# Queueing the modulation's column sums behind the LayerNorms of the sub-layer ahead

## The chip, the cores and the metric

The kernel runs on one core of a Trainium2 chip. The metric is the device time of one execution in microseconds (us); it is given as the median of several executions. The engines are TensorE (PE: matrix products and transposes, PEld its weight loads), VectorE (DVE), ScalarE (ACT), GpSimd (POOL) and SyncE (SP, whose queue issues most DMAs).

## What is computed

An encoder of two layers over 256 positions of width 1024, in float32, with a conditioning vector c. Layer 0 is feed-forward, gMLP, feed-forward; layer 1 is feed-forward, attention (against keys and values that are projected once from the stream), feed-forward. Each of the six sub-layers is, with w = 1/2 for the feed-forwards and 1 for the others,

```
x <- LayerNorm(ALPHA * x + w * gate(c) * f(x * (1 + scale(c)) + shift(c)))
```

`gate`, `scale` and `shift` are vectors of 1024 values each, `c` times columns of a large matrix `w_ada`. They make up twenty such vectors in all, K/V's two among them.

## The kernel before, in words

**Tiles and passes.** The 256 positions are two token tiles, t = 0 and 1, of 128. X[t] holds the residual stream. Every weight comes in pieces of 128 x 1024 in float32 (512 KB) from SP's queue (`load_raw`, L184) into one of six buffers of the pool `raw`. ScalarE makes the rounded part `hi` (L190) and VectorE the rest, `lo` (L191), into 11 `unit` buffers; each product is then three matmuls, `hi` by the activation's high part (L234), `lo` by it (L235), and `hi` by the activation's low part (L237). Only when `lo` has been written is the raw buffer free again. SP issues raw transfers in the program's order, and each waits for a released buffer.

**Columns.** The vectors of the modulation are sums over rows, one *column step* for each of eight pieces of 128 values: `column` (L122) loads 512 KB into the same pool `raw` and has VectorE multiply and reduce it in place, with a short read of the sum behind it. A list of these steps is set for each sub-layer by `ada_phase` (L158); `pump` (L166), called by `prep` (L194) for each weight piece that is prepared, takes steps from it by credits, so that columns lie between weights. Once a gate's eight columns are summed, `finish_gate` (L144) writes the sums to DRAM through POOL and reads them back as a broadcast tile `gate` on SP's queue (`small_dma`, L179).

**A sub-layer's end.** The last pass computes the two 512-wide halves of a tile. `add_y` multiplies a half with the gate (`gy`, L325) and adds it to X[t] (L327 or L330), `rstd_of` takes the statistics (`st` L338, `mv` L340, `rs` L342, and POOL's power, L343), and `normalise` (L346) applies them to both halves of X[t] (L349). The next sub-layer's input follows: TensorE transposes X (`hp`, L300), ScalarE scales and shifts it (`hf`, L288) and rounds it (`hh`, L269), VectorE makes the low part (`hl`, L270). Both tiles do this, tile 1 a little behind tile 0. The affine part of the LayerNorm is applied to X later (L368, L369).

**What sets the order.** No order is written out. The framework's planner takes the program in the order in which it is written as priorities, and puts each engine's instructions in a row by its own costs, by the dependences and by the buffers that are free. `tc.issue_after(i)` adds one more edge: the instructions inside it come behind `i` on the engine of `i`, which here is VectorE. The column steps of sub-layer s+1 begin while the weights of its first pass are prepared, so they reach into the last pass of sub-layer s.

The sub-layers are counted 0 to 5 below: FFN, gMLP, FFN, FFN, attention, FFN. "3 to 4" is the boundary between FFN and attention.

Of the kernel before, what the change touches and what calls it, by code (L numbers as in the profile page):

```python
# [11 lines left out]
ALU = mybir.AluOpType  # L12
# [32 lines left out]
LAG_R = (20, 16)  # L45

N_WARM = 40

COLS = [(0, 1), (0, 0), (0, 4), (0, 3), (0, 7), (0, 6), (1, 1), (1, 0), ("kv", 1), ("kv", 0),
        (1, 4), (1, 3), (1, 7), (1, 6)]  # L50
# [5 lines left out]
def encoder_kernel(ctx, tc, a, out):  # L56
    nc = tc.nc
# [22 lines left out]
    def nm(s):  # L80
        uid[0] += 1
        return f"{s}_{uid[0]}"
# [43 lines left out]
    def col_slice(key):  # L126
        ci = COLS.index(key)
        st = {}

        def step(j):  # L130
            if j == 0:
                st["m"] = modp.tile([P, KD], F32, tag="mod", name=nm("mod"))
            column(ci, j, st["m"])
            if j < KD - 1:
                return
            if ci < N_MODS:
                mods[key] = st["m"]
            else:
                after(LAG_M, lambda: finish_gate(key, st["m"]))
        return [lambda j=j: step(j) for j in range(KD)]  # L140
# [15 lines left out]
    ada = {"steps": [], "credit": 0.0}  # L156

    def ada_phase(*parts):  # L158

        for _, s in ada["steps"]:  # L160
            s()
        ada["steps"] = [(units / (KD * len(keys)), s) for keys, units in parts
                        for k in keys for s in col_slice(k)]
        ada["credit"] = 0.0

    def pump():  # L166
        ada["credit"] += 1.0
        while ada["steps"] and ada["credit"] >= ada["steps"][0][0]:
            cost, s = ada["steps"].pop(0)
            ada["credit"] -= cost  # L170
            s()


    last = {}
# [19 lines left out]
    def prep(srcs):  # L194
        w = split(load_raw(srcs), nc.vector)
        pump()
        return w
# [134 lines left out]
    def pieces(x_, cuts):  # L332
        return [x_[:, c0:c1] for c0, c1 in zip(cuts, cuts[1:])]

    def rstd_of(parts):
        stats = smp.tile([P, len(parts), 6], F32, tag=f"st{len(parts)}", name=nm("st"))
        for i, x_ in enumerate(parts):
            nc.vector.bn_stats(out=stats[:, i, :], in_=x_)  # L338
        mv = smp.tile([P, 2], F32, tag="mv", name=nm("mv"))
        nc.vector.bn_aggr(out=mv, in_=stats)  # L340
        rs = smp.tile([P, 2], F32, tag="rs", name=nm("rs"))
        nc.vector.tensor_scalar(rs[:, 0:1], mv[:, 1:2], EPS, None, op0=ALU.add)  # L342
        nc.gpsimd.tensor_tensor(rs[:, 1:2], rs[:, 0:1], mhalf, op=ALU.pow)  # L343
        return mv[:, 0:1], rs[:, 1:2]

    def normalise(t):  # L346
        mu, rs = rstd_of(pieces(X[t], HALVES))
        for x_ in pieces(X[t], HALVES):
            nc.vector.tensor_scalar(x_, x_, mu, rs, op0=ALU.subtract, op1=ALU.mult)  # L349

    lnrow = {}

# [25 lines left out]
    def end_sublayer(t, ln, nxt):  # L378

        normalise(t)  # L380
        hT[t] = []
        after(LAG_H[t], lambda: make_h(t, 0, nxt["mods"]))

        def second():
            make_h(t, 1, nxt["mods"])
            residual_affine(t, ln)
        after(LAG_H[t] + LAG_H2, second)
# [17 lines left out]
    def first_gu_part(w_gu, part, aT):  # L405
# [10 lines left out]
        warm = pt.tile([P, 512], F32, tag="pt", name=nm("warm"))  # L416
        for i in range(N_WARM):
            nc.tensor.transpose(warm[:, i % 4 * P:(i % 4 + 1) * P], ident, ident)
# [358 lines left out]
    def next_affine(ln, nxt, *keys):  # L777

        def f():
            ada_phase()  # L780
            flush()
            nxt["mods"] = [affine(mods[s_], mods[b_], ln) + dst
                           for (s_, b_), dst in zip(keys, ((htp, "h", hT), (bigp, "b", hkT)))]
            load_lnrow(ln)
        return f

    def step(ln):
# [3 lines left out]
    done, nxt = step(0)  # L791
    ffn(0, 0, (0, 2), done, next_affine(0, nxt, ((0, 4), (0, 3))), PARTS1,
        start=lambda: (ada_phase(([(0, 2)], 13), ([(0, 4), (0, 3)], 24)),))

    done, nxt = step(1)
    ada_phase(([(0, 5)], 16), ([(0, 7), (0, 6)], 22))
    gmlp((0, 5), done, next_affine(1, nxt, ((0, 7), (0, 6))))

# [63 lines left out]
```

## Time and profile before

| | us |
|---|---|
| median of 3 runs | 1055.06 (1053.86 to 1055.79) |
| the profiled execution | 1051.13 |
| its span | 1049.4 |

| engine | busy us | share of the span |
|---|---|---|
| TensorE | 1023.8 | 98% |
| VectorE | 848.0 | 81% |
| ScalarE | 506.1 | 48% |
| DMA engines (mean of 16) | | 77% |

TensorE's row is nearly full, so its stops are what can be shortened. A wait in the profile names the instruction that came last; the duration of an instruction with "xN" holds N of them. TensorE's matmuls overlap: one lists 0.39 us and the next starts 0.23 us later, so a stop is the time from one start to the next less 0.23 us.

### The profile page before, as it was taken

The numbers are of one execution on the slowest core, as the hardware profiler recorded it, in microseconds if no ns is written. First come the engines' busy times: TensorE is split into PE (matmuls) and PEld (weight loads), VectorE is DVE, ScalarE is ACT, GpSimd is POOL, SyncE is SP. The second block draws the span as 40 slices with busy tenths as digits, with TensorE's granted clock in tenths as the row PEclk, the third lists the DMA queues.
The fourth block names the chain that finished last, engine by engine and source line by source line (L and its number), as shares of the span: only waits on it lengthen the run. The fifth ranks groups of instructions, "written<-read, shape, count | busy, mean of one in ns | idle before, by whom it ended". The sixth has DMA issues, their size and how long they took to land.

```text
span 1049.4 us, 13511 instructions
## 1 busy us (share of the span) xinstructions
PE 1023.8 (98%) x4780; PEld 837.2 (80%) x4780; DVE 848.0 (81%) x1227; ACT 506.1 (48%) x710; POOL 22.4 (2%) x39
## 2 busy tenths in 40 slices
PE   8999999999999999999999999999999999999996
PEld 6778878887688788888878888887787788888885
DVE  6877887899999999988679986868998969655535
ACT  3554346462436454454456444453558556355520
POOL 0000000000000100000000000000000000000000
PEclk9999999999999999999999999999999999999999
DMA  8988899688799889999847996767898838645611
GB/s 325 388 324 324 303 361 332 234 277 284 248 344 332 276 279 326 373 348 325 296 149 264 330 349 232 252 242 265 285 341 291 290 102 274 228 161 197 244 61 40
DMA packets 111203, 285.74 MB, mean 272 GB/s; under 512 B 9888, under 2 KB 22560, under 8 KB 111136
## 3 DMA queue, kind: packets, MB, share of 16 engines
q1 hardware_dynamic: 110944, 284.86, 77.3%
q8 instruction: 37, 0.61, 0.2%
q14 instruction: 30, 0.25, 0.1%
q0 software_dynamic: 192, 0.02, 0.0%
HBM read 283.78 MB, written 1.07 MB: 271 GB/s over the span
## 4 chain that ended last, share of the span: by engine, by line
PE 71%; DVE 13%; DMA 7%; issue 4%; ACT 2%; POOL 1%; SPq 0%; POOLq 0%; DVEq 0%; ACTq 0%
PE acc L237 22%; PE acc L234 22%; PE acc L235 22%; DVE lo L191 3%; DMA raw<-w_cols 3%; DVE raw L122 3%; PE tp L276 2%; DMA raw<-ffn_gu 2%; DVE st L338 1%; DVE lo L449 1%; DMA raw<-w_in 1%; POOL rs L343 1%; DVE gy L325 1%; DMA raw<-w_o 1%; PE ob L737 1%
## 5 line engine op out<-in xcount | busy, mean ns | idle before, releaser
L190 ACT CAST hi<-raw 128x1024 fp32r<-128x1024 f32 x328 | 341.7, 1058 | 257.5 <-DMA raw<-ffn_gu 68.9
L191 DVE TENSOR_TENSOR lo<-raw,hi 128x1024 fp32r<-128x1024 f32 x328 | 394.7, 1220 | 54.8 <-ACT hi L190 49.7
L234 PE MATMUL acc<-hi,hh 128*128 128x512 f32 x924 | 359.4, 395 | 3.0 <-ACT hh L466 2.4
L235 PE MATMUL acc<-lo,hh 128*128 128x512 f32 x924 | 355.8, 392 | 5.3 <-DVE lo L191 4.6
L237 PE MATMUL acc<-hi,hl 128*128 128x512 f32 x924 | 291.1, 390 | 0.2 <-DVE hl L270 0.2
L122 DVE CUSTOM_DVE_ANT_0 raw<-raw,c_row,bcol 128x1024 f32<-128x1024 f32 x160 | 204.4, 1278 | 23.4 <-DMA raw<-w_cols 23.1
L235 PEld LDWEIGHTS acc<-lo,hh 128*128 128x128 f32 x924 | 173.0, 188 | 42.7 <-DVE lo L191 7.4
L234 PEld LDWEIGHTS acc<-hi,hh 128*128 128x128 f32 x924 | 173.2, 188 | 42.2 <-ACT hh L466 4.4
L237 PEld LDWEIGHTS acc<-hi,hl 128*128 128x128 f32 x924 | 173.2, 188 | 37.1 <-DVE hl L270 0.8
L234 PE MATMUL acc<-hi,th 128*128 128x512 f32 (+1 forms) x432 | 163.9, 387 | 0.2 <-ACT th L269 0.2
L235 PE MATMUL acc<-lo,th 128*128 128x512 f32 (+1 forms) x432 | 161.9, 383 | 0.1
L237 PE MATMUL acc<-hi,tl 128*128 128x512 f32 (+1 forms) x432 | 143.3, 383 | 0.0
L234 PEld LDWEIGHTS acc<-hi,th 128*128 128x128 f32 x432 | 81.2, 188 | 15.6 <-ACT th L269 0.5
L235 PEld LDWEIGHTS acc<-lo,th 128*128 128x128 f32 x432 | 81.1, 188 | 15.4 <-DVE lo L191 0.5
L237 PEld LDWEIGHTS acc<-hi,tl 128*128 128x128 f32 x432 | 80.6, 188 | 15.9
L395 DVE TENSOR_TENSOR a<-acc,sg 128x512 f32<-128x512 f32 (+1 forms) x48 | 30.9, 643 | 44.3 <-ACT sg L394 44.3
L394 ACT ACTIVATE sg<-acc 128x512 f32<-128x512 f32 (+1 forms) x48 | 27.0, 563 | 82.0 <-PE acc L237 79.9
L288 ACT ACTIVATE hf<-hp,B,A 128x128 f32<-128x128 f32 x96 | 36.7, 477 | 60.3 <-PE hp L300 60.3
L270 DVE TENSOR_TENSOR tl<-tp,th 128x512 fp32r<-128x512 f32 (+1 forms) x56 | 36.2, 649 | 26.5 <-ACT th L269 26.2
L269 ACT CAST th<-tp 128x512 fp32r<-128x512 f32 (+1 forms) x56 | 30.9, 554 | 52.4 <-PE tp L276 52.3
L325 DVE TENSOR_TENSOR gy<-acc,gate 128x512 f32<-128x512 f32 (+1 forms) x49 | 32.0, 675 | 20.5 <-PE acc L237 20.4
L343 POOL TENSOR_TENSOR rs<-rs,mhalf 128x1 f32<-128x1 f32 x14 | 14.7, 1053 | 674.0 <-DVE rs L342 674.0
(93 smaller groups left out, 539.3 us busy)
## 6 DMA issues: line engine op xcount, KB each, us to landing
raw<-w_cols SPq DMA_DIRECT2D x160, 512.0 KB, 5.3
raw<-ffn_gu SPq DMA_DIRECT2D x160, 512.0 KB, 5.5
raw<-ffn_down SPq DMA_DIRECT2D x88, 512.0 KB, 5.3
raw<-w_in SPq DMA_DIRECT2D x32, 512.0 KB, 5.2
raw<-ffn_gu SPq DMA_DIRECT2D x32, 256.0 KB, 4.2
raw<-w_out SPq DMA_DIRECT2D x16, 512.0 KB, 5.7
raw<-w_kv SPq DMA_DIRECT2D x16, 512.0 KB, 5.4
raw<-w_q SPq DMA_DIRECT2D x8, 512.0 KB, 4.7
```

What stands on the lines that cost most here:

```text
L122: nc.vector.tensor_tensor_reduce(out=raw, in0=raw, in1=c_row, scale=1.0, scalar=bcol[:, ci, j:j + 1], op0=ALU.mult, op1=ALU.add, accum_out ...
L190: nc.scalar.copy(hi, raw)
L191: last["lo"] = eng.tensor_tensor(lo, raw, hi.bitcast(F32), op=ALU.subtract)
L234: nc.tensor.matmul(acc, lhsT=xh, rhs=wh[:, sl], start=k == 0, stop=False)
L235: nc.tensor.matmul(acc, lhsT=xh, rhs=wl[:, sl], start=False, stop=False)
L237: nc.tensor.matmul(acc, lhsT=xl, rhs=wh[:, sl], start=False, stop=k == nk - 1)
L269: nc.scalar.copy(hi, src_ps)
L270: nc.vector.tensor_tensor(lo, src_ps, hi.bitcast(F32), op=ALU.subtract)
L288: nc.scalar.activation(hf[:, sl], tp[:, sl], AF.Identity, bias=B[:, j:j + 1], scale=A[:, j:j + 1])
L325: nc.vector.tensor_tensor(tmp, acc[:, :c1 - c0], g[:, sl], op=ALU.mult)
L394: nc.scalar.activation(sg[:, :wd], g, AF.Silu)
L395: nc.vector.tensor_tensor(av[:, :wd], u, sg[:, :wd], op=ALU.mult)
```

## The change

Column steps of a sub-layer get an extra edge, once the first sub-layer's LayerNorms have been recorded: the first two steps stand behind the second `normalise` instruction of tile 0 of the sub-layer ahead, all others behind that of tile 1. A counter of the steps is added to `ada_phase`, and `normalise` records its last instruction. The edge orders VectorE's reductions; the columns' transfers keep their places on SP.

```
+N_EARLY = 2
...
-        ada["credit"] = 0.0
+        ada["credit"], ada["n"] = 0.0, 0
...
             cost, s = ada["steps"].pop(0)
             ada["credit"] -= cost
-            s()
+            with ExitStack() as es:
+                if ("ln", 1) in last:
+                    es.enter_context(tc.issue_after(last["ln", ada["n"] >= N_EARLY].ins))
+                s()
+            ada["n"] += 1
...
         for x_ in pieces(X[t], HALVES):
-            nc.vector.tensor_scalar(x_, x_, mu, rs, op0=ALU.subtract, op1=ALU.mult)
+            last["ln", t] = nc.vector.tensor_scalar(x_, x_, mu, rs, op0=ALU.subtract, op1=ALU.mult)
```

The lines that follow are the planned rows of the engines. L-numbers are higher by two to six with the change, since lines were added. In the rows, a column is the `ISA` with `raw` and `mod`, with its short read behind it.

VectorE at tile 0's LayerNorm between sub-layers 1 and 2, before (X0 is the tile's stream, `st`, `mv` and `rs` its statistics):

```order
L122 ISA raw_710_3197,mod_694_3140<-raw_710_3197,c_row_102,bcol_108 128x1024
L122 ISA mod_694_3140 128x1
L340 BN_AGGR mv_669_3019<-st_668_3016 128x2
L122 ISA raw_714_3212,mod_694_3140<-raw_714_3212,c_row_102,bcol_108 128x1024
L122 ISA mod_694_3140 128x1
L342 TENSOR_SCALAR rs_670_3021<-mv_669_3019 128x1
L191 TENSOR_TENSOR lo_702_3168<-raw_700_3165,hi_701_3167 128x1024
L349 TENSOR_SCALAR X0_105<-X0_105,mv_669_3019,rs_670_3021 128x512 x2
L191 TENSOR_TENSOR lo_709_3194<-raw_707_3191,hi_708_3193 128x1024
```

and with the change:

```order
L346 BN_AGGR mv_669_3019<-st_668_3016 128x2
L348 TENSOR_SCALAR rs_670_3021<-mv_669_3019 128x1
L355 TENSOR_SCALAR X0_105<-X0_105,mv_669_3019,rs_670_3021 128x512 x2
L124 ISA raw_695_3141,mod_694_3140<-raw_695_3141,c_row_102,bcol_108 128x1024
L124 ISA mod_694_3140 128x1
L124 ISA raw_699_3156,mod_694_3140<-raw_699_3156,c_row_102,bcol_108 128x1024
L124 ISA mod_694_3140 128x1
L197 TENSOR_TENSOR lo_702_3168<-raw_700_3165,hi_701_3167 128x1024
```

Columns that stood between the statistics now stand behind the two instructions that normalise X0, and they are the first two of the gate's eight, 695 and 699; 710 and 714, which are later ones, are further down.

VectorE at tile 1's LayerNorm between sub-layers 3 and 4, before (`mod_1437` is the gate of the attention, `mod_1492` the vector after it, X1 tile 1's stream):

```order
L191 TENSOR_TENSOR lo_1469_6497<-raw_1467_6494,hi_1468_6496 128x1024
L340 BN_AGGR mv_1426_6362<-st_1425_6359 128x2
L191 TENSOR_TENSOR lo_1473_6512<-raw_1471_6509,hi_1472_6511 128x1024
L342 TENSOR_SCALAR rs_1427_6364<-mv_1426_6362 128x1
L191 TENSOR_TENSOR lo_1491_6619<-raw_1489_6616,hi_1490_6618 128x1024
L349 TENSOR_SCALAR X1_106<-X1_106,mv_1426_6362,rs_1427_6364 128x512 x2
L122 ISA raw_1493_6623,mod_1492_6622<-raw_1493_6623,c_row_102,bcol_108 128x1024
L122 ISA mod_1492_6622 128x1
L191 TENSOR_TENSOR lo_1496_6635<-raw_1494_6632,hi_1495_6634 128x1024
```

and with the change:

```order
L197 TENSOR_TENSOR lo_1469_6497<-raw_1467_6494,hi_1468_6496 128x1024
L348 TENSOR_SCALAR rs_1427_6364<-mv_1426_6362 128x1
L355 TENSOR_SCALAR X1_106<-X1_106,mv_1426_6362,rs_1427_6364 128x512 x2
L124 ISA raw_1446_6412,mod_1437_6381<-raw_1446_6412,c_row_102,bcol_108 128x1024
L124 ISA mod_1437_6381 128x1
L124 ISA raw_1450_6427,mod_1437_6381<-raw_1450_6427,c_row_102,bcol_108 128x1024
L124 ISA mod_1437_6381 128x1
L124 ISA raw_1458_6456,mod_1437_6381<-raw_1458_6456,c_row_102,bcol_108 128x1024
L124 ISA mod_1437_6381 128x1
L276 TENSOR_TENSOR hl_1454_6447<-hf_1452_6441,hh_1453_6446 128x512
L124 ISA raw_1462_6471,mod_1437_6381<-raw_1462_6471,c_row_102,bcol_108 128x1024
L124 ISA mod_1437_6381 128x1
```

One column of the next vector stood behind the normalise before; now six of the gate's stand there, four of them shown, and the low parts `lo_1473` and `lo_1491`, which stood ahead of it, come after five and six of them.

TensorE at the same boundary, before (`hp_1451` and `hp_1463` are the transposes of X1, `acc_1432` and `acc_1433` the accumulators of the key projection of tile 0):

```order
L237 MATMUL acc_1432_6373<-hi_1460_6467,hl_1057_4733 128x512
L237 MATMUL acc_1433_6374<-hi_1460_6467,hl_1057_4733 128x512
L234 MATMUL acc_1432_6373<-hi_1468_6496,hh_1056_4732 128x512
L235 MATMUL acc_1432_6373<-lo_1469_6497,hh_1056_4732 128x512
L234 MATMUL acc_1433_6374<-hi_1468_6496,hh_1056_4732 128x512
L235 MATMUL acc_1433_6374<-lo_1469_6497,hh_1056_4732 128x512
L237 MATMUL acc_1432_6373<-hi_1468_6496,hl_1057_4733 128x512
L237 MATMUL acc_1433_6374<-hi_1468_6496,hl_1057_4733 128x512
L234 MATMUL acc_1432_6373<-hi_1472_6511,hh_1056_4732 128x512
L235 MATMUL acc_1432_6373<-lo_1473_6512,hh_1056_4732 128x512
L300 MATMUL hp_1451_6436<-ident_109,X1_106 128x128 x4
L300 MATMUL hp_1463_6480<-ident_109,X1_106 128x128 x4
```

and with the change:

```order
L243 MATMUL acc_1432_6373<-hi_1456_6452,hl_1057_4733 128x512
L243 MATMUL acc_1433_6374<-hi_1456_6452,hl_1057_4733 128x512
L240 MATMUL acc_1432_6373<-hi_1460_6467,hh_1056_4732 128x512
L306 MATMUL hp_1451_6436<-ident_109,X1_106 128x128 x4
L241 MATMUL acc_1432_6373<-lo_1461_6468,hh_1056_4732 128x512
L240 MATMUL acc_1433_6374<-hi_1460_6467,hh_1056_4732 128x512
L241 MATMUL acc_1433_6374<-lo_1461_6468,hh_1056_4732 128x512
L243 MATMUL acc_1432_6373<-hi_1460_6467,hl_1057_4733 128x512
L243 MATMUL acc_1433_6374<-hi_1460_6467,hl_1057_4733 128x512
L306 MATMUL hp_1463_6480<-ident_109,X1_106 128x128 x4
L240 MATMUL acc_1432_6373<-hi_1468_6496,hh_1056_4732 128x512
```

The transposes of X1 stand two weight pieces earlier on TensorE than before: ahead of the products with `lo_1461`, where they stood among those with `hi_1472`.

## Rows read from the trace of the kernel before

**Rows 1.** The page: busy time of the engines, and the last chain by engine.

```profile
PE 1023.8 (98%) x4780; PEld 837.2 (80%) x4780; DVE 848.0 (81%) x1227; ACT 506.1 (48%) x710; POOL 22.4 (2%) x39
...
PE 71%; DVE 13%; DMA 7%; issue 4%; ACT 2%; POOL 1%; SPq 0%; POOLq 0%; DVEq 0%; ACTq 0%
```

**Rows 2.** Waits of TensorE: engine, line, waited for, total us, times, longest.

```profile
PE acc L235 <- DVE lo L191: 4.6, 3, 1.9
...
PE hp L300 <- DVE X L349: 2.5, 6, 0.8
...
PE acc L234 <- ACT hh L269: 0.2, 1, 0.2
PE acc L237 <- DVE hl L270: 0.2, 1, 0.2
```

**Rows 3.** Timeline of TensorE at 1 to 2: start, duration, instruction, idle before.

```profile
351.76 0.39 PE L234 MATMUL acc<-hi,th 128*128 128x512 f32 x1
352.74 1.09 PE L300 MATMUL hp<-ident,X 128*128 128x128 f32 x8 [0.59 <-DVE X L349]
```

**Rows 4.** Groups by line of VectorE: count, busy us, mean ns, idle before.

```profile
L191 DVE TENSOR_TENSOR lo<-raw,hi 128x1024 fp32r<-128x1024 f32 x328 | 394.7, 1220 | 54.8 <-ACT hi L190 49.7
L122 DVE CUSTOM_DVE_ANT_0 raw<-raw,c_row,bcol 128x1024 f32<-128x1024 f32 x160 | 204.4, 1278 | 23.4 <-DMA raw<-w_cols 23.1 <-DVE c_row L415 0.2
```

**Rows 5.** Waits of SP's own queue.

```profile
SPq L184 <- DVE lo L191: 261.6, 188, 11.9
...
SPq L184 <- DVE mod L122: 135.9, 99, 6.4
```

**Rows 6.** The page: DMA issues of the column buffers, last figure us to landing.

```profile
raw<-w_cols SPq DMA_DIRECT2D x160, 512.0 KB, 5.3
```

**Rows 7.** Busy time by stretch: PE, PEld, DVE, ACT, POOL, clock, DMA share.

```profile
213.00:252.00 39.00, 39.00 (x177) 32.38 (x178) 38.84 (x57) 18.65 (x27) 1.58 (x2) 1.00 0.90 301
757.00:782.00 25.00, 24.27 (x115) 19.75 (x114) 23.93 (x34) 12.43 (x18) 0.00 (x0) 1.00 1.00 358
```

**Rows 8.** Timeline of TensorE at 0 to 1.

```profile
256.50 0.72 PE L235 MATMUL acc<-lo,hh 128*128 128x512 f32 x2 [1.75 <-DVE lo L191]
```

**Rows 9.** Timeline of VectorE at 1 to 2.

```profile
340.95 1.28 DVE L122 CUSTOM_DVE_ANT_0 raw<-raw,c_row,bcol 128x1024 f32<-128x1024 f32 x1
...
349.07 1.28 DVE L122 CUSTOM_DVE_ANT_0 raw<-raw,c_row,bcol 128x1024 f32<-128x1024 f32 x1 [0.40 <-DMA raw<-w_cols]
...
350.29 0.15 DVE L342 TENSOR_SCALAR rs<-mv 128x1 f32<-128x1 f32 x1
...
352.04 1.00 DVE L349 TENSOR_SCALAR X<-X,mv,rs 128x512 f32<-128x512 f32 x2 [0.44 <-POOL rs L343]
```

**Rows 10.** Timeline of VectorE at 2 to 3.

```profile
551.98 1.00 DVE L349 TENSOR_SCALAR X<-X,mv,rs 128x512 f32<-128x512 f32 x2 [0.45 <-POOL rs L343]
552.89 3.49 DVE L191 TENSOR_TENSOR lo<-raw,hi 128x1024 fp32r<-128x1024 f32 x3
```

**Rows 11.** Timeline of ScalarE at 2 to 3.

```profile
555.00 0.64 ACT L269 CAST hh<-hf 128x512 fp32r<-128x512 f32 x1
```

**Rows 12.** Timeline of VectorE at 3 to 4.

```profile
726.12 1.00 DVE L349 TENSOR_SCALAR X<-X,mv,rs 128x512 f32<-128x512 f32 x2 [0.75 <-POOL rs L343]
728.60 1.28 DVE L122 CUSTOM_DVE_ANT_0 raw<-raw,c_row,bcol 128x1024 f32<-128x1024 f32 x1 [1.48 <-DMA raw<-w_cols]
...
742.75 1.00 DVE L349 TENSOR_SCALAR X<-X,mv,rs 128x512 f32<-128x512 f32 x2 [0.46 <-POOL rs L343]
```

**Rows 13.** Timeline of TensorE at 3 to 4.

```profile
725.59 0.39 PE L234 MATMUL acc<-hi,th 128*128 128x512 f32 x1
726.81 0.63 PE L300 MATMUL hp<-ident,X 128*128 128x128 f32 x4 [0.83 <-DVE X L349]
```

**Rows 14.** Timeline of SP's queue at 3 to 4.

```profile
722.26 0.33 SPq L184 DMA_DIRECT2D raw<-w_kv  x1
...
733.43 0.33 SPq L179 DMA_DIRECT2D gate<-grow  x1
```

## The prediction, made before the changed kernel was run

> **What bounds the kernel now.** I read five views in this order. First the page's busy shares and its chain: TensorE has an instruction under way for 98% of the span, and 71% of the chain that ended last runs through it, 13% through VectorE and 7% through transfers [rows 1]. So a change counts only where TensorE stands still, before or after. Second, TensorE's waits: of those that a LayerNorm can cause, the page has 2.5 us in six waits of the transposes `hp` for X, 0.2 us for `hh` and 0.2 us for `hl` [rows 2]; the larger entry, 4.6 us in three waits, is for a weight's low part `lo`. Each stop also costs about 0.16 us of refilling (at 351.76 the next start is 0.98 us later; 0.59 of that is the wait and 0.23 the usual step, [rows 3]), for about nine stops 1.4 us. So **the most that an earlier LayerNorm can give back is 2.9 + 1.4 = 4.3 us.** Third, VectorE's groups: 328 low parts at 1.22 us and 160 column sums at 1.28 us [rows 4]. Fourth, what the DMA queue on SP waits for: mostly for a buffer that a low part or a column sum must release, 261.6 us and 135.9 us for weights alone [rows 5]. A buffer is thus re-filled as soon as VectorE has read it, and with 5.3 us from issue to landing [rows 6] a buffer that is read late brings the weight after next late. Fifth, the timelines at each LayerNorm, below.
>
> The profiled execution took 1051.13 us, 3.93 us under the median of the timed runs (1055.06) and 1.7 us over its span. I sum against the profiled execution and add 3.93 at the end.
>
> **The change part by part.** No instruction is added or removed. At five sub-layer boundaries columns that stood among the statistics go behind the LayerNorm of tile 0 (two of each sub-layer) or of tile 1 (the rest). The transfers stay in nearly the same order on SP; what moves is when a column releases its buffer, and what TensorE's and ScalarE's schedule was built around it.
>
> FFN0 to gMLP. Tile 0's LayerNorm gains two steps, but TensorE had no wait there. Behind tile 1's LayerNorm stands one column more. From 213 to 252 us VectorE is busy for 38.84 of 39.00 us [rows 7], so the 1.28 us pass undiminished to the low part for which TensorE stands still for 1.75 us at 256.50 [rows 8]. Low end 0 (the weight's own transfer turns out to be the limit), high end 1.5 (the column and its read, and a little re-filling). I take **+1.2**, VectorE's step for a column.
>
> gMLP to FFN1. Here is the gain. From 340.95 to 349.07 four columns stand between X and its `rs`; the LayerNorm starts at 352.04 [rows 9], 4 x 1.2 = 4.8 us later than need be, and TensorE stands 0.75 us over its step [rows 3], followed by about 0.8 us for `hh`, `hl` (the three refills and the 0.4 of waits). All 1.6 us go. Behind tile 1 the four columns come due together; the weight loaded into a buffer that they or the late low parts hold lands about 5 us after its release, ScalarE casts it in front of `hf` of tile 1, and by my reckoning `hh` is ready 0.6 us after TensorE wants it. Net **-1.0**, ends -1.4 and +0.3.
>
> FFN1 to FFN2. Before, TensorE waited only 0.16 us for tile 1's X. Now two columns stand between the normalise, which starts at 551.98, and the three low parts that follow it at once [rows 10]: 2 x 1.2 us. The planner therefore lets TensorE go to tile 1's units early; they need `hh`, which ends at 555.00 + 0.64 = 555.64 [rows 11], while TensorE runs out of tile 0's work near 554.6: 1.05 us. A further low part, five columns further back, comes some 0.6 us late. **+1.5**, ends 0 (the two low parts were early enough) and +2.2.
>
> FFN2 to attention is the largest. All eight columns of a gate fall into the FFN's last pass; before, the eighth started at 728.60 [rows 12]. Tile 0's LayerNorm comes 2.6 us sooner, so TensorE's 0.99 us between 725.59 and 726.81 (1.22 less the step of 0.23) vanishes [rows 13]: **-1.0.** But with six buffers, the columns now wait unread in up to four of them. The weights of `w_kv` that SP issued up to 722.26 [rows 14] find none; the first late one goes out near 727, the next near 732, lands near 737, and its low part stands ahead of `rs` in VectorE's queue. The LayerNorm of tile 1, before at 742.75, so stays near 741.5 to 742. In the new order TensorE meets `hp` of tile 1 13 matmuls earlier, near 739: it stands for 2.7 us where before it stood for 0.36. Six columns then run 6 x 1.2 = 7.2 us ahead of the next low parts, but some of the other small stops there go (0.4). Up to here the sum is -1.0 + 2.7 - 0.4 - 0.4 = +0.9. Behind it, the eighth column ends near 752, 22 us later than before, and the gate's load on SP, before at 733.43 [rows 14], comes near 756 and is waited for in front of the weights of `w_q`. VectorE is then about 9 us behind in a stretch where it is busy for 23.93 of 25.00 us [rows 7] and can catch up 1 us; four of the low parts of the value projection come 0.5 to 1.0 us late, of which part was already a wait for ScalarE: I take 0.9 of these 3. Together **+1.8**, ends -0.6 (the weights land early enough and only the gain and a first small loss stay) and +4 (all of it).
>
> A rule of the Trainium skill bears on this place. Its page "Perfetto Trace Analysis", under Identifying Performance Opportunities, says that gaps which repeat on the engine that should be full can mean that there is no SBUF left for the next tile. It speaks against holding six buffers longer; SP's 261.6 us of waiting for a low part [rows 5] is the row on it, and by it the high end of this boundary would be the likely one.
>
> How long a buffer is dark is the second such place. The row says 5.3 us from issue to landing of 512 KB [rows 6], and I use that. The Trainium skill's page "DMA: Bandwidth & Descriptors", under Anatomy of one DMA, gives, for transfers that GpSimd issues, about 2.0 us and the bytes at 436 GB/s: by it a column lands in 3.2 us (an estimate), the stop of 2.7 us shrinks to 0.6, and the sum below would be 2.1 us less. The trace does not agree, with 2.1 us more.
>
> Attention to FFN3. Five columns move, two behind tile 0 and three behind tile 1, ahead of one `hl` that was just as late before and of low parts with some 10 us of lead. **+0.3**, ends -0.5 (half a microsecond of tile 1's `hp` wait goes) and +1.
>
> Sum: 1.2 - 1.0 + 1.5 + 1.8 + 0.3 = **+3.8 us**: 1054.9 for a profiled execution, 1058.9 on the median's scale.
>
> **The rivals.** *The LayerNorms win.* The waits for X, `hh` and `hl` go at all boundaries, 4.3 us, and the late buffers stay hidden because weights are cast many units ahead of use: 1055.06 - 4.3 = 1050.8. For it: VectorE is idle for 19% of the span. Against it: not at these places [rows 7], and it needs tile 1's LayerNorm to be earlier, where the order now lets low parts wait for weights. It decides from the point where the re-filled weight at 727 lands before 733. Chance 0.15 (faster).
>
> *It comes out even.* Gains of about 2.6 (the two larger stops for X with their `hh` and `hl`) against losses of as much, or the moved columns fall into slack: within 2.1 us of 1055. TensorE's waits that the change can touch are few [rows 2], which speaks for it; the losses appear in places that had no wait before, which speaks against. Chance 0.27.
>
> *The buffers run dry.* At the attention boundary VectorE does not catch up at all: the high ends there and at the two FFN boundaries, 4 + 2.2 + 1.5 + 1 with the 0.3 on the gain's side, 9 us: 1064. For it: SP's waits [rows 5] and the two DMA-bound stretches; against: TensorE had only 4.6 us of waits for low parts in the whole run [rows 2], so low parts lead comfortably. Chance 0.14.
>
> *The forecast*, +3.8 with its own range of +2.1 to +6: chance 0.44.
>
> **How the numbers follow.** A measurement of this kernel tells about 0.2%, 2.1 us, from no change. Faster 0.15, within 0.27, slower 0.44 + 0.14 = 0.58. The likeliest gives 1058.9, the range 1053 to 1064: its low end takes in the even case and half of the gain, its high end the dry buffers.
>
> **What would show it.** Right: no stop of TensorE near 352 and 726, the gaps at `hp` of the FFN1 and attention boundaries replaced by a longer one near 739 (waiting for X) and one near 555 (waiting for `hh`); the low part at 256 about a microsecond later; SP waiting for `mod` of a column where it waited for low parts; the gate's load about 22 us later. Wrong: tile 1's LayerNorm of the attention boundary starting before 739, or no wait for `lo` after it; then the raw buffers were not the limit and the first rival holds. If the stop near 739 is over 4 us, the third does.

## The result, and the profile after

The changed kernel takes 1061.20 us in the median of four runs (1060.28 to 1062.31), the kernel before on the same chip 1054.46 (1051.48 to 1055.79). The ratio is 1.0058, 95% interval [1.0039, 1.0077], or 6.1 us: slower, inside the forecast range, on the forecast side, 2.3 us over the forecast of 1058.9 and just past the +2.1 to +6 us that the prediction gave to the forecast alone. One execution of the kernel with ten raw buffers (below) took 2657.40 us and is left out of every figure.

The page after, busy time of the engines. [rows 1] has it before.

```profile
PE 1028.7 (97%) x4780; PEld 839.1 (79%) x4780; DVE 850.3 (80%) x1227; ACT 507.1 (48%) x710; POOL 20.7 (2%) x39
```

The work is the same; TensorE's 98% became 97%. TensorE's waits after, with the columns of [rows 2]:

```profile
PE acc L241 <- DVE lo L197: 10.6, 11, 3.1
...
PE hp L306 <- DVE X L355: 2.5, 5, 1.2
...
PE acc L240 <- ACT hh L275: 1.9, 3, 0.9
PE acc L241 <- DVE rs L348: 1.0, 1, 1.0
```

The transposes still wait 2.5 us for X, as before. The waits for a low part went from 4.6 us in three places to 10.6 in eleven (and one of 1.0 us more that the profile puts to `rs`), those for `hh` from 0.2 to 1.9. So TensorE's waits for X did not shrink in the sum, and most of what it waits longer is for low parts.

Where it arose can be read from a comparison of the two traces: the start of the same matmul after, less its start before, is its lag (taken as the median over 10 us). The lag is 0.37 us at 190, 4.17 at 330, 5.75 at 430, 8.82 at 580, 7.76 at 730, 11.43 at 800, 10.63 at 850 and 11.30 at 880, where it stays. These two executions lie 11.2 us apart (1062.31 against 1051.13), since the one is the slowest of its runs and the other below the median of its own; the medians lie 6.7 us apart. The steps of the lag therefore tell places, and the timed runs below tell sizes. Even as places they need repeating: over a boundary where a kernel has no edge, the lag of its single trace moved by up to some 3 us (in the runs below, `ln0_24` by 3.2 from 190 to 330 and `b3` by 2.8 from 330 to 430).

**FFN0 to gMLP, 3.8 us of lag.** TensorE after, in the gMLP (start, duration, instruction, idle before), answering [rows 8]:

```profile
257.90 0.74 PE L241 MATMUL acc<-lo,hh 128*128 128x512 f32 x2 [1.04 <-DVE rs L348]
...
265.60 1.22 PE L241 MATMUL acc<-lo,hh 128*128 128x512 f32 x2 [3.10 <-DVE lo L197]
```

VectorE at the same place, before and after. Before:

```profile
263.04 2.35 DVE L191 TENSOR_TENSOR lo<-raw,hi 128x1024 fp32r<-128x1024 f32 x2
265.31 1.28 DVE L122 CUSTOM_DVE_ANT_0 raw<-raw,c_row,bcol 128x1024 f32<-128x1024 f32 x1
```

After:

```profile
263.13 1.28 DVE L124 CUSTOM_DVE_ANT_0 raw<-raw,c_row,bcol 128x1024 f32<-128x1024 f32 x1
...
264.33 2.36 DVE L197 TENSOR_TENSOR lo<-raw,hi 128x1024 fp32r<-128x1024 f32 x2
```

A column stands in front of the two low parts for which TensorE waits, where it stood behind them: the planner, given the edges, has put columns and low parts in another order 50 us behind the LayerNorm. VectorE itself is not late here. Its statistics of V begin at 254.12, before at 254.04, and wait for ScalarE both times. A second thing follows the stop; the stretch behind it, with the columns of [rows 7]:

```profile
264.50:271.50 7.00, 5.90 (x14) 4.65 (x15) 7.00 (x9) 1.05 (x1) 0.00 (x0) 0.51 0.82 258
```

The granted clock is 0.51 there, the lower of its two levels (1.2 of 2.4 GHz), behind a stop of 3.10 us. In the kernel before the longest stop here was 1.9 us, and the granted clock of 260 to 268 us was 1.00. A dozen matmuls step 0.43 us where 0.23 is usual: some 2.5 us of the lag.

**gMLP to FFN1, 1.6 us.** Tile 0's transposes no longer wait (compare [rows 3]), and its LayerNorm is early ([rows 9]): it began at 350.59 in a run that lagged by 4.2 us. The lag falls by 1.7 us, to 2.5 at 360, and is lost again. Tile 1's `hp` and the `hh` behind it are late:

```profile
367.43 0.66 PE L306 MATMUL hp<-ident,X 128*128 128x128 f32 x4 [0.43 <-DVE X L355]
...
372.19 0.50 PE L240 MATMUL acc<-hi,hh 128*128 128x512 f32 x1 [0.65 <-ACT hh L275]
```

Two shorter waits follow, 0.67 us for a low part at 403.58 and 0.34 us for a high part at 424.43.

**FFN1 to FFN2, 3.1 us.** TensorE after:

```profile
561.43 0.50 PE L240 MATMUL acc<-hi,hh 128*128 128x512 f32 x1 [0.86 <-ACT hh L275]
...
571.31 0.73 PE L241 MATMUL acc<-lo,hh 128*128 128x512 f32 x2 [1.18 <-DVE lo L197]
```

VectorE there, answering [rows 10]:

```profile
557.72 1.00 DVE L355 TENSOR_SCALAR X<-X,mv,rs 128x512 f32<-128x512 f32 x2 [0.44 <-POOL rs L349]
558.64 1.28 DVE L124 CUSTOM_DVE_ANT_0 raw<-raw,c_row,bcol 128x1024 f32<-128x1024 f32 x1
...
568.22 1.28 DVE L124 CUSTOM_DVE_ANT_0 raw<-raw,c_row,bcol 128x1024 f32<-128x1024 f32 x1 [1.73 <-DMA raw<-w_cols]
...
570.03 3.49 DVE L197 TENSOR_TENSOR lo<-raw,hi 128x1024 fp32r<-128x1024 f32 x3
```

Two columns, at 558.64 and 559.84, stand between the normalise and the next low part, as the order had said; the wait for `hh` of 0.86 us and its refilling is the 1.05 us forecast. The second stop is the larger one: at 568.22 a column waits 1.73 us for its own transfer, and the low parts stand behind it.

**FFN2 to attention, 1.8 us.** TensorE after, answering [rows 13]:

```profile
734.39 0.60 PE L306 MATMUL hp<-ident,X 128*128 128x128 f32 x4
...
749.21 0.66 PE L306 MATMUL hp<-ident,X 128*128 128x128 f32 x4 [1.23 <-DVE X L355]
...
772.83 0.50 PE L241 MATMUL acc<-lo,hh 128*128 128x512 f32 x1 [0.75 <-DVE lo L197]
...
776.50 0.73 PE L241 MATMUL acc<-lo,hh 128*128 128x512 f32 x2 [1.50 <-DVE lo L197]
```

The stop at tile 0's LayerNorm is gone (the transposes at 734.39 do not wait), then tile 1's X costs 1.4 us and two low parts of `w_q` 2.7 (by the starts, less the usual step). ScalarE and SP's queue show why, ScalarE first:

```profile
745.51 1.05 ACT L196 CAST hi<-raw 128x1024 fp32r<-128x1024 f32 x1 [2.83 <-DMA raw<-w_kv]
...
770.47 1.05 ACT L196 CAST hi<-raw 128x1024 fp32r<-128x1024 f32 x1 [3.19 <-DMA raw<-w_q]
```

SP's queue after, answering [rows 14]:

```profile
722.05 0.33 SPq L190 DMA_DIRECT2D raw<-w_kv  x1
734.70 0.33 SPq L123 DMA_DIRECT2D raw<-w_cols  x1
735.91 0.33 SPq L190 DMA_DIRECT2D raw<-w_kv  x1
...
759.22 0.33 SPq L123 DMA_DIRECT2D raw<-w_cols  x1
764.71 0.33 SPq L185 DMA_DIRECT2D gate<-grow  x1
765.14 0.37 SPq L190 DMA_DIRECT2D raw<-w_q  x1
```

Between 722.05 and 734.70 SP issues nothing: every raw buffer holds a column that may not be read before X0 is normalised, or a weight. The weight issued at 741.09 is the one that ScalarE waits for at 745.51, and its low part is in front of tile 1's `rs`. Tile 1's LayerNorm itself is not later than before:

```profile
748.61 1.00 DVE L355 TENSOR_SCALAR X<-X,mv,rs 128x512 f32<-128x512 f32 x2 [0.73 <-POOL rs L349]
```

Less the lag of 8.8 us at this boundary that is 739.8, and before it was 742.75 [rows 12]; but TensorE's order had moved the transposes still further forward. The second gap, 759.22 to 764.71, is SP waiting until the gate's sums have landed in DRAM; the weight behind it is the one for which ScalarE waits 3.19 us at 770.47 and TensorE after that. Before, the gate went out at 733.43.

### The profile page after: what moved, and what is told of

Read it like the earlier page. It is cut to its first block, busy times and chain, and to the rows that moved or that the text cites. A ratio compares the mean times of both kernels' runs of the same rounds, so it can differ in the third digit from the quotient of the medians.

```text
span 1060.5 us, 13497 instructions
## 1 busy us (share of the span) xinstructions
PE 1028.7 (97%) x4780; PEld 839.1 (79%) x4780; DVE 850.3 (80%) x1227; ACT 507.1 (48%) x710; POOL 20.7 (2%) x39
## 4 chain that ended last, share of the span: by engine, by line
PE 55%; DVE 10%; DMA 6%; issue 3%; ACT 3%; POOL 0%; POOLq 0%; SPq 0%; DVEq 0%; ACTq 0%
PE acc L241 17%; PE acc L243 17%; PE acc L240 17%; DVE lo L197 3%; DVE raw L124 3%; DMA raw<-ffn_down 1%; PE tp L282 1%; DMA raw<-ffn_gu 1%; ACT hi L196 1%; DMA raw<-w_cols 1%; DMA raw<-w_in 1%; PE ob L743 1%; DVE gy L331 1%; DVE hl L276 1%; DMA raw<-w_q 1%
```

## The experiments

Two reasons could make columns behind a LayerNorm cost time. *Buffers*: an unread column keeps one of six raw buffers, so the weights behind it are issued late. *Queue*: the columns come in a bunch in VectorE's own order, ahead of low parts that TensorE wants. The sizes below are the ratio to the kernel before, times its median of 1054.7 us (1054.5 to 1054.9 in the different groups), each with its interval.

### One boundary at a time

A counter of the sub-layer is added to `ada_phase`, and the edge is there for one sub-layer only.

```
+        ada["sub"] += bool(parts)
...
-                if ("ln", 1) in last:
+                if ada["sub"] in SUBS:      # SUBS = (1,), (2,), (3,) or (4,)
```

> The edges at the boundary FFN0 to gMLP alone; at the other four the kernel before. If the costs are local and add up (my theory), this one costs what TensorE lost there in the trace of the changed kernel: 0.36 us at the LayerNorms and 3.1 us in the gMLP, of which some 2.5 us were a stretch of 6 us at the lower granted clock behind a stop of 3.3 us; so +1 us if the clock stays up and +3.5 us if it falls. If the loss comes from the interplay of the boundaries (rival: work that one boundary puts off meets the next), it is within 0.5 us of before.

> The edges at gMLP to FFN1 alone. Local theory: the stop for tile 0's X and the hh and hl behind it go (-1.4 us by 360), tile 1's X and hh are late (+1.4), and low parts are late some 50 us further on (+1.9): in sum +1 to +2 us, with waits for lo near 400 and 424 that before does not have. My prediction had -1.0 here. Rival (the late low parts near 400 come from the delay inherited from the gMLP, not from this boundary): -0.5 to 0 and no waits near 400.

> The edges at FFN1 to FFN2 alone. Local theory: +3.0 us, made of a stop of about 1.0 us for hh of tile 1, one of 1.3 us for a low part some 10 us later and 0.4 us for another. Rival (the stops only appear since the timing is shifted by 5.75 us there): under 1 us.

> The edges at FFN2 to attention alone. Local theory: -1.06 us at tile 0's LayerNorm, then a stop of 1.4 us for tile 1's X, two of 1.0 and 1.7 us for low parts of w_q, later ones in the value projection, less a wait for pTs that goes: +1.8 us. Rival (interplay): the gain of 1 us stays and the stops shrink, -1 to 0.

| boundary | ratio | interval | us |
|---|---|---|---|
| FFN0 to gMLP | 1.0021 | [0.9998, 1.0043] | +2.2 |
| gMLP to FFN1 | 0.9993 | [0.9977, 1.0009] | -0.7 |
| FFN1 to FFN2 | 1.0026 | [1.0002, 1.0050] | +2.7 |
| FFN2 to attention | 1.0018 | [1.0004, 1.0033] | +1.9 |

The sum is 6.1 us, the loss of the whole change (the fifth boundary was not run alone). With intervals of about 2 us on each term it agrees with costs that are local and add up, but does not show it. The interplay rival falls for the fourth by its time, and for the third by its trace, where both stops are back (its interval alone reaches down to 0.2 us). The first can't be told from nothing: its trace has the stop of 3.1 us and the lower clock again (0.66 from 266 to 271), but `ln0_24` below, which has no edge at this boundary, lags as much there. With FFN1 to FFN2 alone:

```profile
558.59 0.50 PE L242 MATMUL acc<-hi,hh 128*128 128x512 f32 x1 [0.85 <-ACT hh L277]
...
568.26 0.74 PE L243 MATMUL acc<-lo,hh 128*128 128x512 f32 x2 [0.94 <-DVE lo L199]
```

With FFN2 to attention alone:

```profile
743.70 0.66 PE L308 MATMUL hp<-ident,X 128*128 128x128 f32 x4 [1.64 <-DVE X L357]
...
771.15 0.72 PE L243 MATMUL acc<-lo,hh 128*128 128x512 f32 x2 [1.44 <-DVE lo L199]
```

At gMLP to FFN1 the local theory missed: I expected +1 to +2 us with waits at 400 and 424. One wait is left near 400 (0.50 us) and none near 424, and the lag is the same at 430 as at 330 (2.0), where the whole change rose by 1.6. That the rest came from the delay that this boundary inherited is argued, not shown.

### Which of the two edges

`ln0` puts all columns behind tile 0's LayerNorm and none behind tile 1's; `ln0_24` does so at gMLP to FFN1 and FFN2 to attention alone.

```
-                    es.enter_context(tc.issue_after(last["ln", ada["n"] >= N_EARLY].ins))
+                    es.enter_context(tc.issue_after(last["ln", 0].ins))
```

> At all five boundaries every column step stands behind tile 0's LayerNorm, none behind tile 1's. If the loss comes from the edge to tile 1's LayerNorm (columns that hold buffers for some 16 us more and then come in a bunch), this loses less than half of the changed kernel's 6.5 us, at FFN2 to attention it keeps the 1 us of tile 0's stop and the gate's load comes 15 us earlier than with the change: 1052 to 1057. If any holding of the columns out of the last pass costs (the buffers of tile 0's wait alone), it stays at 1059 to 1062.

> The edge to tile 0's LayerNorm alone, and only at gMLP to FFN1 and FFN2 to attention, the two places where TensorE stood 0.75 and 0.99 us for tile 0's X. If the tile-1 edge is the cause of the loss, this one keeps the gains and is at or up to 2.5 us below the kernel before, 1052 to 1055; if columns that stand behind the LayerNorm are late for the weights' buffers whatever the edge, it is 1 to 4 us above it.

`ln0`: 1.0013 [0.9995, 1.0031], +1.4 us. `ln0_24`: 0.9970 [0.9950, 0.9990], -3.2 us, at 1052.50 us (2.2 below by the medians). So without the edge to tile 1's LayerNorm most of the 6.1 us are gone, and the other alone, at two places, is a gain. The lag over FFN2 to attention falls by 0.9 us in both, where it rose by 1.8 with the change and by 2.4 with that boundary alone. TensorE with `ln0_24` has no wait at tile 0's transposes and a shorter one at tile 1's:

```profile
729.39 0.60 PE L308 MATMUL hp<-ident,X 128*128 128x128 f32 x4
...
745.07 1.11 PE L308 MATMUL hp<-ident,X 128*128 128x128 f32 x8 [0.65 <-DVE X L357]
```

SP's queue with `ln0_24`, to be read beside that of the change:

```profile
717.29 0.33 SPq L192 DMA_DIRECT2D raw<-w_kv  x1
729.70 0.33 SPq L124 DMA_DIRECT2D raw<-w_cols  x1
...
750.77 0.33 SPq L124 DMA_DIRECT2D raw<-w_cols  x1
755.62 0.33 SPq L187 DMA_DIRECT2D gate<-grow  x1
```

Both gaps of the change are here too, 12.4 and 4.9 us long, in a kernel that gains: neither gap is by itself the loss. The gate's load did not come 15 us earlier either, as I had expected of `ln0`: there it goes out at 757.09, which is 752.0 on the time of before, against 755.9 with the change. What differs is behind the first gap. The next three weights of `w_kv` go out 1.2, 3.6 and 7.2 us after its end (with the change 1.2, 6.4 and 13.1), since the columns between them are read behind tile 0's LayerNorm and not behind tile 1's.

At FFN1 to FFN2 `ln0` still loses, by 3.8 us of lag where the whole change lost 3.1; there the edge to tile 0's LayerNorm alone is enough. Its VectorE:

```profile
543.71 1.28 DVE L124 CUSTOM_DVE_ANT_0 raw<-raw,c_row,bcol 128x1024 f32<-128x1024 f32 x1 [2.57 <-DMA raw<-w_cols]
```

and its TensorE:

```profile
553.40 1.22 PE L241 MATMUL acc<-lo,hh 128*128 128x512 f32 x2 [3.83 <-DVE lo L197]
```

The column at 543.71 waits 2.57 us for its transfer, in the middle of what leads to the next low part (552.13), and TensorE stands 3.83 us, with the granted clock at 0.62 from 552 to 556 behind that. Before it stood 1.0 us there, at a clock of 1.00:

```profile
549.18 0.73 PE L235 MATMUL acc<-lo,hh 128*128 128x512 f32 x2 [0.98 <-DVE lo L191]
```

A column moved behind a LayerNorm is no help where the LayerNorm was not waited for.

### More raw buffers

Eight raw buffers, for ten pairs of split weights (the two pools together keep their size), with the change and without it.

```
-N_RAW = 6
-N_UNIT = 11
+N_RAW = 8
+N_UNIT = 10
```

> The change with eight buffers for raw pieces in place of six, paid for by ten pairs of split weights in place of eleven. To be read against the kernel before with the same pools. If the columns cost because they hold buffers that the weights need, the distance to that kernel falls from 6.5 us to 2 us or less, and the stops for low parts at FFN1 to FFN2 (1.3 us) and in w_q (1.0 and 1.7 us) go. If they cost since they stand in a bunch in VectorE's queue ahead of low parts (rival), the distance stays 4 to 6 us.

> The kernel before with eight raw buffers and ten pairs, the measure for the run with the change and the same pools. Both theories: within 3 us of the kernel before, since TensorE's waits for low parts there are 4.6 us in all; below it if the buffers limit that kernel too, above it if the eleventh pair is needed.

With the change 0.9981 [0.9968, 0.9995], without it 0.9943 [0.9921, 0.9965] (1049.69 us). The distance is 4.0 us by the ratios and 3.5 by the medians, where it was 6.1: at the low edge of what the queue reason expected and above the 2 us of the buffers, and with some 2 us of interval on each ratio the fall itself is not clear of noise. The times thus don't decide between the two.

The kernel before gained 6.0 us [3.7, 8.3], and I had expected 3 at most. More than half of it is won ahead of the first boundary that has an edge: its lag against six buffers is -3.1 us at 190, that of the five other kernels with eight or ten raw buffers -3.3 to -4.0, and that of the seven other kernels with six -0.5 to +1.3. TensorE's waits for low parts did not get fewer (6.2 us in four places; 4.6 in three with six buffers).

At FFN1 to FFN2 there is one stop with the change and one without it, of equal length; first with:

```profile
549.59 0.73 PE L241 MATMUL acc<-lo,hh 128*128 128x512 f32 x2 [2.34 <-DVE lo L197]
```

and without:

```profile
544.93 0.73 PE L235 MATMUL acc<-lo,hh 128*128 128x512 f32 x2 [2.34 <-DVE lo L191]
```

The edges cost nothing here any more (the lag between the two is 4.7 at 430 and at 580), and the two stops of the change with six buffers are gone. But the stop that both have is longer than before (0.98 us at 549.18, above), the granted clock behind it is 0.76 without the change (548 to 552), and the kernel before with eight buffers loses 2.5 us here against itself with six. So that the buffers were the cost at this boundary is not shown.

At FFN2 to attention tile 0's X cost 0.73 us and tile 1's 0.45 without the change:

```profile
725.43 0.63 PE L300 MATMUL hp<-ident,X 128*128 128x128 f32 x4 [0.73 <-DVE X L349]
...
739.72 0.66 PE L300 MATMUL hp<-ident,X 128*128 128x128 f32 x4 [0.45 <-DVE X L349]
```

With it only tile 1's is left, and one low part:

```profile
743.39 0.65 PE L306 MATMUL hp<-ident,X 128*128 128x128 f32 x4 [0.36 <-DVE X L355]
...
766.45 0.50 PE L241 MATMUL acc<-lo,hh 128*128 128x512 f32 x1 [0.47 <-DVE lo L197]
```

There the lag between the two falls by 2.0 us (4.7 at 710, 2.6 at 850), where it had risen by 1.8 with six buffers. In the gMLP it rises by 3.4 us, as with six (3.4 from 240 to 330): TensorE with the change,

```profile
260.66 1.22 PE L241 MATMUL acc<-lo,hh 128*128 128x512 f32 x2 [4.56 <-DVE lo L197]
```

and without,

```profile
260.69 0.73 PE L235 MATMUL acc<-lo,hh 128*128 128x512 f32 x2 [2.87 <-DVE lo L191]
```

Part of this is the clock again: with the change it is 0.57 from 260 to 264 us, without it 1.00 (but see the last section). So at FFN2 to attention the cost went with the buffers: `r8_b4` and `r8_no1` below, which have its edges too, fall there by 1.9 and 1.6 us of lag, and `b1` to `b3`, which have none there, stay within 0.4. In the gMLP the cost stayed. The queue reason is seen there with six buffers (the column in front of the low parts), but with eight no column stands right before the low part of 260.66, so what moves the gMLP's stops there is left open. With both kernels the pools changed the order that the planner finds, so this is shown for the two orders as they came out, not for the size of the pool alone.

### What stays with eight buffers

Four more kernels. `r8_b4` has the change's edges at FFN2 to attention alone, `r8_no1` at all but FFN0 to gMLP, `r8_ln0_24` the tile-0 edge at two places, all with eight raw buffers; `before_raw10` is the kernel before with `N_RAW = 10` and `N_UNIT = 9`.

```
+SUBS = (4,)            # r8_b4
+SUBS = (2, 3, 4, 5)    # r8_no1
+SUBS = (2, 4)          # r8_ln0_24, with last["ln", 0]
```

> Eight raw buffers and ten pairs, and the change's edges at all boundaries but FFN0 to gMLP. The change with eight buffers stood 3.5 us above the same pools without it, and its trace lost 2.7 us of that in the gMLP, where VectorE has no idle time and one more column stands behind tile 1's LayerNorm. If that column in VectorE's queue is the rest of the loss, this is at 1049.5 to 1051; if the rest lies at the other boundaries, at 1052 to 1053.5.

> Eight raw buffers and ten pairs, and the change's edges at FFN2 to attention alone. With six buffers this boundary cost 2.2 us. If it was the buffers, it is now a gain, as the trace of the change with eight buffers has it between 720 and 820 us (-1.1): 1048 to 1050, against 1049.7 without the edges. If the bunch of six columns in VectorE's queue costs by itself (rival), 1051 to 1052.

> Eight raw buffers and ten pairs, and the edge to tile 0's LayerNorm alone at gMLP to FFN1 and FFN2 to attention, which gained 2.2 us with six buffers. If the two gains are of different waits they add up: 1047 to 1048.5. If the edge only helped since six buffers were scarce, it is at 1049.7 or above.

> The kernel before with ten raw buffers and nine pairs of split weights. If raw buffers still limit at eight, 1 to 3 us below eight (1046.5 to 1048.5); if eight are enough, equal; if nine pairs are too few for the weights that two token tiles share, above 1051.

| kernel | median us | ratio | interval |
|---|---|---|---|
| before, 8 buffers | 1049.69 | 0.9943 | [0.9921, 0.9965] |
| `r8_b4` | 1049.06 | 0.9937 | [0.9914, 0.9960] |
| `r8_no1` | 1050.70 | 0.9949 | [0.9929, 0.9968] |
| change, 8 buffers | 1053.15 | 0.9981 | [0.9968, 0.9995] |
| `r8_ln0_24` | 1051.92 | 0.9968 | [0.9951, 0.9986] |
| before, 10 buffers | 1053.48 | 0.9983 | [0.9968, 0.9999] |

`r8_no1` came as expected: without the edges at FFN0 to gMLP the change costs 0.6 us with eight buffers, so 3.4 of the 4.0 us that were left are that boundary, by the ratios, whose intervals are about 2 us to each side. `r8_b4` is the lowest median, but can't be told from eight buffers alone (-0.6 us by the ratios, with some 3 us of interval); by its time and its lag, the loss of 1.9 us at that boundary with six buffers is not there.

`r8_ln0_24` lies over 3 us above the first of its two expectations; the second came, at 1049.7 or above. With eight buffers the two gains don't add up. TensorE at FFN2 to attention has the stop for tile 0's X no more, but new ones:

```profile
738.92 0.72 PE L243 MATMUL acc<-lo,hh 128*128 128x512 f32 x2 [0.46 <-DVE lo L199]
...
761.68 1.14 PE L653 MATMUL tp<-ident,k 128*128 128x128 f32 x8 [2.60 <-ACT k L650]
```

A low part is late (738.92) in a stretch with five columns behind tile 0's LayerNorm, and the transposes of `k` wait 2.60 us where they waited 1.72 without the edge. In sum this boundary neither gains nor loses: the lag against the kernel before with eight buffers is 2.8 at 710 and at 850. The trace lost its time earlier, 1.4 us at gMLP to FFN1 (1.5 at 330, 2.9 at 430) and 1.7 in the gMLP, where it has no edge. Why, I did not take apart.

Ten buffers are worse than eight. Which of the two sizes does it was not tried apart; the waits of TensorE for low parts are 12.6 us in two entries:

```profile
PE acc L235 <- DVE lo L191: 9.0, 7, 4.3
PE acc L235 <- DVE rs L342: 3.6, 1, 3.6
```

## Why the prediction was right, point by point

The sign came out and, at FFN2 to attention, the reason for it: columns that wait for a LayerNorm keep buffers, and the weights behind them come late. The sizes came out in part. FFN1 to FFN2 measured about twice its term, FFN2 to attention has the right number without the parts that I gave for it, and the first two terms can't be told from nothing by their own runs. That the sum is as near as it is has luck in it.

**The ceiling of the gain** (4.3 us) held: what the edges gave back at tile 0's LayerNorms was 1.7 us of lag at gMLP to FFN1 and 1.06 at FFN2 to attention, for which I had 1.6 and 1.0. Tile 1's waits were not given back. The ceiling was read from one execution, with nine stops where [rows 2] has eight; `b3` and `b4`, which have no edge at gMLP to FFN1, stood 1.96 and 1.41 us there for tile 0's X where that execution stood 0.59.

**FFN0 to gMLP, +1.2.** 2.2 us by the run alone [-0.2, +4.5] and 3.8 of lag, and the step failed in its mechanism. The column's 1.28 us were not passed on: VectorE waits for ScalarE at 254 us (2.12 us before, 1.55 after), which took them up. In their place came a column in front of the awaited low parts, by the planner's new order, and a stretch at the lower clock level. My high end of 1.5 was too low for either. How much of it the edges cause is not shown with six buffers; with eight, leaving out this boundary's edges saves 3.4 us (`r8_no1`).

**gMLP to FFN1, -1.0.** The run alone gives -0.7 [-2.4, +0.9], which holds the forecast but can't be told from nothing; in the whole change the lag rose by 1.6. `hh` of tile 1 was 0.65 us late, where I had 0.6; the late `hp` of tile 1 and the two waits at 403 and 424 I did not have.

**FFN1 to FFN2, +1.5.** The term that was most mis-sized: 2.7 by the run alone, 3.1 of lag. The first part, 1.05 us for `hh`, is there almost to the digit. The second, "some 0.6 us", was 1.3 us, since the column in front of the low parts itself waited for a buffer and then for its transfer. I had counted the columns' time in VectorE's queue, and of the late transfers only those of weights.

**FFN2 to attention, +1.8.** 1.9 by the run alone, 1.8 of lag, but not of the parts that I gave: here the number is luck. Tile 0's gain is there. Tile 1's X cost 1.4 us in place of 2.7, since its LayerNorm began at 739.8 on the time of before and not at 741.5 to 742. Two low parts of `w_q` cost 2.7, for which I had nothing before the value projection, and two waits for `k` (0.79 and 0.73 us before) went. In the value projection the waits that came and the wait for `pTs` that went nearly cancel. The gate's load came at 764.71, which is 755.9 on the time of before, as worked out (756). What it delayed was SP's queue, which stood 5.5 us for it, and not VectorE; but `ln0_24` stood 4.9 us for it and gained.

**Attention to FFN3, +0.3.** 0.7 of lag; not run alone.

**The rivals.** That the LayerNorms win fell by the time, although tile 1's LayerNorm at the attention boundary did start 2.9 us earlier than before, as that rival needed: TensorE met it earlier still. That it comes out even fell by the interval. The dry buffers were the nearest rival: the mechanism is the one that the runs show at FFN2 to attention, and the true loss lies between it and the forecast. The sentence that low parts "lead comfortably" was wrong; three waits before became eleven. The rule of the Trainium skill's page "Perfetto Trace Analysis", Identifying Performance Opportunities, that gaps which repeat can mean too little SBUF, agrees with the times here: two more raw buffers for one split pair less made the kernel before 6.0 us faster (0.9943), more than any order of the columns did. The traces agree less: the waits for low parts did not get fewer, and over half of the gain lies ahead of 190 us.

## What to carry to other kernels

Work that holds a shared buffer should not be queued behind a late event, even if its engine has time: what it costs is the transfer that the buffer can't take, and that is seen tens of microseconds later on another engine (FFN2 to attention is where the runs show it). To bring a critical chain forward, one edge at the places where it is waited for (`ln0_24`) did better than a rule for all places with six buffers; with eight the same edge made the kernel 2 to 3 us slower, so an order is good for one set of pools. Before the order is tuned, the sizes of the pools are worth a run: a trade of one split pair for two raw buffers beat both kernels, and a second such trade lost most of it.

## What the runs showed of the hardware that was not expected

A stop of 3.10 us of TensorE in the gMLP was followed by a stretch at the lower granted clock (0.51 from 264.5 to 271.5), some 2.5 us of lag; in the kernel before, with a stop of 1.9 us there, it was 1.00. But the length of the stop does not settle it. Four kernels with eight buffers and no edge at FFN0 to gMLP have the same stop of 2.87 us near 260: behind it the clock of 260 to 264 was 1.00 in two of them (the kernel before, `r8_no1`) and 0.60 and 0.73 in the others (`r8_b4`, `r8_ln0_24`). So the time of one execution holds some 2 us of chance, and the clock's part of the loss in the gMLP can't be put down to the edges. The row of `r8_b4` (columns as in [rows 7]):

```profile
260.00:264.00 4.00, 3.83 (x10) 3.06 (x11) 4.00 (x6) 1.03 (x1) 0.00 (x0) 0.60 0.86 284
```

And a transfer on SP's queue that waits for a write to DRAM (the gate, 759.22 to 764.71) holds up all weights behind it. The kernel before has such waits too: 23.4 us in its six gates, 27.7 with the change.
